# The last expert block's rows added on chip, and the last norm ahead of the overflow loop

## The chip, the cores and the metric

One core of a Trainium2 chip. The time is device microseconds for one execution of the whole program. Most executions of one kernel agree within 0.3%. Engines are TensorE (PE; its weight loads are PEld), VectorE (DVE), ScalarE (ACT), GpSimd (POOL) and SyncE (SP, which only issues DMAs here). DMAs are issued from the queues of SP, ScalarE and GpSimd.

## What is computed

One layer of a streaming encoder over 576 rows of 1024 channels: 512 rows of a new stream and 64 of a running one. After the token mixing and a first norm, each row is routed to two of 16 experts. The part that matters here is the end of it:

```
gl  = hf @ w_group + b_group ; g = argmax            # one group of 4 experts per row
top = top_k(router logits in the group, 2)           # two experts per row
act = silu(gate) * up * combine                      # each expert: 1024 -> 2 x 256
y   = sum over the row's two experts of act @ w_down # 256 -> 1024
x   = LayerNorm(ALPHA * x + (1 + g2) * y) * ln2_g + ln2_b
```

Everything is f32. The other outputs (keys, values, convolution state) are written long before.

## The kernel before

The 576 rows stand in five tiles of 128 rows (`TS` = 128, 128, 128, 128, 64). A scratch tensor in DRAM, `z_scr` (`z_d`), first receives ALPHA times the normed rows (`ax_rows`, line 888), and each expert's output is then added to it row by row.

**Units.** The experts are worked off by `units` (line 1276 on): four fixed ones, then nine by the string "mhhsmsmsm". Each letter stands for experts in order of how many rows they have: "h" is one expert in two blocks of 128 rows, "m" one expert in one block, "s" two small experts that share a block, 64 rows each. For each block `gather` fetches the rows with an indirect DMA, `rows_in` transposes them, `gate_up` multiplies them in four steps, `hidden` makes the activation. Within a loop over the units the block before is finished inside the steps of the present one: `turned` transposes the activation, `down` (lines 1175 and 1179) multiplies it with `w_down` into two PSUM banks `pd`, and `add_rows` (line 1182) multiplies by the gate on VectorE (line 1186, tile `yo`) and adds the result to `z_scr` by an indirect accumulating DMA from GpSimd (line 1190), whose row numbers stand in `idt`, `ido` or `cols`. A block of an "s" unit issues two of them, one for each expert; there are 18 in all. Each waits until the one before has landed, because rows of different experts may be the same rows.

**Buffers.** Seven large slots (`slot`) rotate: six hold the ring of expert weights, one the transposed rows `xhl`. What is allocated after them, as `rows3` (the last norm's gain and bias, line 1475), takes the slot of the oldest weights when those have been read.

**Order.** Inside `tc.manual_schedule` the order on TensorE, VectorE and ScalarE is the order in which the code is written; SP and GpSimd, and everything behind that block, are ordered by a planner with a timing model. An engine's instructions run in that order.

**The end.** After the last unit `turn_next` and `product_next` finish the pending block. Then comes the overflow loop (`tc.For_i`, line 1484), for experts that got more rows than their blocks hold. Its count is a value read at run time; in the profiled execution it is zero, and no line of its body is in the trace. Its entry and exit on every engine are checks of semaphores and branches. Behind the loop, for each of the five tiles: SP loads `zt` from `z_scr` (line 1515), the statistics are taken on VectorE for tile 0 (`stats`, `bn_stats` at line 804) and on ScalarE for the others (`act_stats`: a copy with a sum at line 1505, a square with a sum at 1507, a root at 1508, a reciprocal on VectorE at 1509), two VectorE passes (1517 and 1518) subtract the mean, multiply by gain and the inverse deviation and add the bias, and SP stores the tile (1519). The program's end has line 1560.

Of the kernel before, what the change touches and what calls it, by code (L numbers as in the profile page):

```python
# [10 lines left out]
F32 = mybir.dt.float32  # L11
# [3 lines left out]
AF = mybir.ActivationFunctionType  # L15
OP = mybir.AluOpType
AX = mybir.AxisListType

D = 1024
# [5 lines left out]
NT = 5  # L25
TS = [128, 128, 128, 128, 64]
# [14 lines left out]
NFIX = 4  # L41
# [8 lines left out]
def dap(a, offset, ap):  # L50
    return bass.AP(tensor=a.tensor, offset=a.offset + offset, ap=ap)
# [7 lines left out]
def encoder_step(ctx: ExitStack, tc: tile.TileContext, a, o):  # L59
    nc = tc.nc  # L60
    V, S, G, PE, SY = nc.vector, nc.scalar, nc.gpsimd, nc.tensor, nc.sync

    def scratch(name, shape, dt=F32):
        return nc.dram_tensor(name, shape, dt).ap()
# [4 lines left out]
    z_d = scratch("z_scr", (T, D))  # L69
# [7 lines left out]
    def slot(shape, dt=F32, name="slot"):  # L77
        return big.tile(shape, dt, name=name, tag="slot", padded_shape=None)
# [19 lines left out]
    ident = cst.tile([128, 128], F32, name="ident")  # L98
# [9 lines left out]
    epst = cst.tile([128, 1], F32, name="epst")  # L108
# [188 lines left out]
    class AdaRows:  # L297
# [12 lines left out]
        def product(self):  # L310
            k = self.done
            self.done += 1
            if k == 0:
                self.p = fifth(self.name)
            for j in range(4):
                PE.matmul(self.p[32 * j:32 * j + 32, :], cT[:, k, :], self.ws[k // 2][:, k % 2, 512 * j:512 * j + 512],
                          start=k == 0, stop=k == KT - 1, tile_position=(0, 32 * j))
# [12 lines left out]
    def fm(src, ncols, c0, xh, xl, m=128):  # L330
        with tc.high_priority(offset=400):
            raw = wcols(src, ncols, c0, m)
            ada_next("load")
            with tc.issue_after(hlast):
                w = split(raw, [128, KT, m])
        ps = [acc(), acc()]
        ada_next("product")
        for h in range(2):
            for k in range(KT):
                fm_step(ps, w, h, k, xh, xl, m)  # L340
        return ps
# [110 lines left out]
    def tm(c0, n, kstep):  # L452
        ps = [(acc, acc, acc, dot, fifth)[t](f"tm{t}") for t in range(NT)]
        for k0 in range(0, KT, kstep):
            with tc.high_priority():
                raw = wload(dap(a["w_in"], k0 * 128 * NIN + c0, [[NIN, 128], [128 * NIN, kstep], [1, n]]),
                            [128, kstep, n])
                wh, wl = split(raw, [128, kstep, n])
            order = [(k, t) for k in range(k0, k0 + kstep) for t in range(NT)]
            if k0 + kstep == KT:  # L460
                order = [(k, t) for t in range(NT) for k in range(k0, KT)]
            tokens_product(ps, k0, kstep, hh, hl, hs, wh, wl)
        return ps
# [25 lines left out]
    ps = fm(a["w_in"], NIN, C_KI, hh, hl, 72)  # L489
# [8 lines left out]
    for kv, t0, t1, n in ((kip, 0, 4, 128), (kis, 4, 5, DEC)):  # L498
        src = pki[0:n, 72 * t0:72 * t1].rearrange("p (t c) -> p t c", t=t1 - t0)
# [10 lines left out]
    ps = tm(C_QI, 512, 2)  # L510
    for t in range(NT):
        n = TS[t]
# [32 lines left out]
    ps = tm(C_K, 512, 2)  # L545
    for t in range(NT):
        n = TS[t]
# [17 lines left out]
    for c in range(2):  # L565
        ps = tm(C_Q + 512 * c, 512, 2)
        for t in range(NT):
            n = TS[t]
# [33 lines left out]
    bias = {0: bias0}  # L602
# [147 lines left out]
    late = ctx.enter_context(tc.tile_pool(name="late", bufs=2))  # L750


    def brow(dst, src, off, eng=G):
        eng.dma_start(dst, dap(src, off, [[0, 128], [1, D]]))
# [46 lines left out]
    def stats(src, n):  # L801
        bs = late.tile([128, 2, 6], F32, name="bs", tag="bs", bufs=2)
        for c in range(2):
            V.bn_stats(bs[0:n, c, :], src[0:n, 512 * c:512 * c + 512])
        mv = late.tile([128, 4], F32, name="mv", tag="mv", bufs=NT)
        V.bn_aggr(mv[0:n, 0:2], bs[0:n])
        S.activation(mv[0:n, 2:3], mv[0:n, 1:2], AF.Sqrt, bias=epst[0:n])
        V.reciprocal(mv[0:n, 2:3], mv[0:n, 2:3])
        return mv[0:n, 0:1], mv[0:n, 2:3]
# [3 lines left out]
    iota128 = late.tile([128, 128], F32, name="iota128", bufs=1)  # L813
# [35 lines left out]
    ps = [(acc, acc, acc, dot, fifth)[t](f"o{t}") for t in range(NT)]  # L849
# [117 lines left out]
    for t in range(NT):  # L967
        n = TS[t]
# [54 lines left out]
    for j in range(2):  # L1023
        V.tensor_tensor(Ej[:, j], Ej[:, j], bc(w12[:, :, j], 16), op=OP.mult)
        for t in range(NT):
            n = TS[t]
            PE.matmul(pwt[:, 0:16], ohr[0:n, j, t, :].bitcast(F32), Ej[0:n, j, t, :], start=t == 0 and j == 0,
                      stop=t == NT - 1 and j == 1)
# [6 lines left out]
    with tc.issue_after(routed):  # L1035
# [17 lines left out]
        cols = late.tile([128, 2, NVAR], F32, name="cols", bufs=1)  # L1053
# [94 lines left out]
    def hidden(p, w):  # L1148
        hm = late.tile([128, DE], F32, name="hm", tag="hm", bufs=3)
        S.activation(hm, p[:, 0:DE], AF.Silu)  # L1150
        V.scalar_tensor_tensor(hm, hm, w, p[:, DE:2 * DE], op0=OP.mult, op1=OP.mult)
        return hm

    def turned(hm):
        pt = fifth("pht")
        for i in range(2):
            PE.transpose(pt[:, 128 * i:128 * i + 128], hm[:, 128 * i:128 * i + 128], ident)
        hT = late.tile([128, 2, 128], F32, name="hT", tag="hT", bufs=2)
        S.copy(hT, pt[:, 0:256].rearrange("p (k t) -> p k t", k=2))  # L1159
        return hT  # L1160

    def gate_row(s0, s1):
        y = wp.tile([128, D], F32, name="yo", tag="wraw", bufs=2) if len(scatters) % 3 else \
            late.tile([128, D], F32, name="yo", tag="xg", bufs=2)
        S.activation(y, gr1, AF.Copy, scale=s1)
        V.scalar_tensor_tensor(y, gr0, s0, y, op0=OP.mult, op1=OP.add)
        return y
# [15 lines left out]
    def add_rows(y, pd_, ids):  # L1183
        for c in range(2):
            cs = slice(512 * c, 512 * c + 512)
            V.tensor_tensor(y[:, cs], y[:, cs], pd_[c], op=OP.mult)

        for i, idx in enumerate(ids):
            half = slice(128 // len(ids) * i, 128 // len(ids) * (i + 1))
            sc = G.indirect_dma_start(out=z_d, out_offset=bass.IndirectOffsetOnAxis(ap=idx[0:128 // len(ids)], axis=0),  # L1190
                                      in_=y[half], in_offset=None, bounds_check=T - 1, oob_is_err=False, compute_op=OP.add)
        scatters.append(sc.ins)
# [80 lines left out]

    plan = [[u] for u in range(NFIX)]
    nxt_ = {"h": 0, "m": NPAIR, "s": NFULL}
    for kind in "mhhsmsmsm":
        r = nxt_[kind]
        nxt_[kind] += 1
        plan.append([NFIX + r] + ([NFIX + r + NHALF] if kind == "s" else []))
    units, nb = [], 0  # L1280
    for es in plan:
        x = Unit()
# [12 lines left out]
    for u, x in enumerate(units):  # L1295
        x.experts = []
        for e in x.es:
            y = Expert()
# [67 lines left out]
    with tc.manual_schedule(engines={mybir.EngineType.PE, mybir.EngineType.DVE, mybir.EngineType.Activation}):  # L1366
# [4 lines left out]
        pend, over = [], overflow()  # L1371
# [10 lines left out]
        for u, x in enumerate(units):  # L1382
            if u == 2:
                for y in units:
                    i = y.es[0] - NFIX
# [8 lines left out]
            for b, _ in x.blocks:  # L1394
                p = Unit()
# [42 lines left out]
            def turn_next(i):  # L1438
                if i < len(pend):
                    pend[i].hT = turned(pend[i].hm)  # L1440

            def product_next(i):
                if i < len(pend):
                    product(pend[i])

            if len(blocks) == 1:
                p = blocks[0]
# [10 lines left out]
            else:  # L1458
                p, q = blocks
# [14 lines left out]
            pend = blocks  # L1474
        rows3 = slot([128, 2, D], name="rows3")
        brow(rows3[:, 0], a["ln2_g"], 0, SY)
        brow(rows3[:, 1], a["ln2_b"], 0, SY)
        for i in range(len(pend)):
            turn_next(i)
            product_next(i)  # L1480

    nvals = nc.values_load_multi_w_load_instructions(ovi[0:1, 2 * NOV:2 * NOV + 1], min_val=0, max_val=NOV,
                                                     skip_runtime_bounds_check_because="bounded by the counts")[1]
    with tc.For_i(0, nvals[0], 1) as i:
# [11 lines left out]
            load_down(ev, k, wt[1][:, k, :])  # L1496
        y = gate_row(s0, s1)
        add_rows(y, down(turned(hidden(pg, w)), [[wt[1][:, k, :] for k in range(2)]]), ids)


    jk = slot([128, D], name="jk")

    def act_stats(src, n):
        mv = late.tile([128, 4], F32, name="mv", tag="mv", bufs=NT)
        S.activation(jk[0:n], src[0:n], AF.Copy, scale=1.0 / D, accum_out=mv[0:n, 0:1])
        V.tensor_scalar(mv[0:n, 3:4], mv[0:n, 0:1], -1.0, None, op0=OP.mult)
        S.activation(jk[0:n], src[0:n], AF.Square, bias=mv[0:n, 3:4], accum_out=mv[0:n, 1:2])
        S.activation(mv[0:n, 2:3], mv[0:n, 1:2], AF.Sqrt, bias=epst[0:n], scale=1.0 / D)
        V.reciprocal(mv[0:n, 2:3], mv[0:n, 2:3])
        return mv[0:n, 0:1], mv[0:n, 2:3]  # L1510

    for t in range(NT):
        n, s = TS[t], int(t == 4)
        zt = slot([128, D], name="zt")
        SY.dma_start(zt[0:n], dap(z_d, t * 128 * D, [[D, n], [1, D]]))
        mean, rs = stats(zt, n) if t == 0 else act_stats(zt, n)
        V.scalar_tensor_tensor(zt[0:n], zt[0:n], mean, rows3[0:n, 0], op0=OP.subtract, op1=OP.mult)
        V.scalar_tensor_tensor(zt[0:n], zt[0:n], rs, rows3[0:n, 1], op0=OP.mult, op1=OP.add)
        SY.dma_start(dap(o["y"][s], (t % 4) * 128 * D, [[D, n], [1, D]]), zt[0:n])


# [42 lines left out]
```

## Time and profile before

| | us |
|---|---|
| median of 3 runs | 874.6 |
| lowest and highest | 872.26, 875.77 |
| the profiled execution's own time | 876.71 |
| its span | 875.0 |
| TensorE busy | 791.9 (90%) |
| VectorE busy | 640.5 (73%) |
| ScalarE busy | 358.6 (41%) |
| GpSimd busy | 143.6 (16%) |

The span is what the hardware profiler records; 1.7 us of the execution's time lie around it. Busy shares are averages over stages with different limits. The tail from about 830 us on is a stage of its own: there the chain of waits (at each step the thing that released the next) and the table by stretches say more than the shares. The mean granted clock of TensorE over the span is 0.95 of full speed.

### The profile page before, as it was taken

What the parts mean: (1) busy time and instruction counts of PE and PEld (TensorE: products, weight loads), DVE (VectorE), ACT (ScalarE), POOL (GpSimd) and SP (SyncE); (2) the same over time, 40 slices, a digit from 0 to 9 for tenths busy, and PEclk for the clock granted to TensorE, in tenths of its full rate; (3) what the DMA queues carried; (4) which work ended last, traced back from release to release, by engine and by line L of the source; (5) the groups of instructions that cost most, each with busy time, mean ns of one, the idle gap of its engine ahead of it and who ended that gap; (6) DMA issues with size and microseconds to landing.
All of it is one profiled execution on the core that took longest, in us unless ns stands there. A gap on an engine that the chain in (4) does not pass through costs nothing.

```text
span 875.0 us, 13257 instructions
## 1 busy us (share of the span) xinstructions
PE 791.9 (90%) x4827; PEld 640.9 (73%) x4827; DVE 640.5 (73%) x1255; ACT 358.6 (41%) x654; POOL 143.6 (16%) x172
## 2 busy tenths in 40 slices
PE   4899999999999999999999999799947999999920
PEld 3788888887878879879899789788836667645400
DVE  1569999989999889988896425437797697555516
ACT  3243232324344335547743852222433564344205
POOL 2300000310200000000100001020257532322220
PEclk9999999999999999999999999899956999999975
DMA  9997664491423224232443105677597999799525
GB/s 289 342 352 254 204 201 126 120 246 56 148 75 89 83 75 115 89 100 62 135 127 106 54 1 194 224 214 260 116 273 242 346 348 316 200 335 386 149 46 201
DMA packets 108866, 159.70 MB, mean 183 GB/s; under 512 B 9715, under 2 KB 67211, under 8 KB 108801
## 3 DMA queue, kind: packets, MB, share of 16 engines
q1 hardware_dynamic: 94464, 120.38, 42.1%
q0 software_dynamic: 12736, 34.26, 15.3%
q10 hardware_dynamic: 1600, 4.22, 1.3%
q8 instruction: 38, 0.62, 0.3%
q14 instruction: 28, 0.22, 0.1%
HBM read 143.65 MB, written 26.13 MB: 194 GB/s over the span
## 4 chain that ended last, share of the span: by engine, by line
PE 58%; DVE 7%; DMA 7%; issue 2%; ACT 2%; POOL 1%; POOLq 0%; SPq 0%; DVEq 0%; ACTq 0%
PE acc L242 7%; PE acc L244 7%; PE acc L243 7%; PE pd L1175 4%; PE pdot L528 3%; PE pg L1145 2%; DMA wraw<-in_w_att_out_dram 2%; PE tm L144 2%; PE tm L146 2%; PE tm L145 2%; PE pl L652 2%; PE po L660 2%; PE pg L144 2%; DMA z_scr<-yo,idt 2%; PE pg L146 2%
## 5 line engine op out<-in xcount | busy, mean ns | idle before, releaser
L588 DVE SCALAR_TENSOR_TENSOR y<-ue,dwT,y 128x604 f32<-128x604 f32 (+17 forms) x232 | 183.2, 828 | 1.9 <-ACT y L586 1.5
L242 PE MATMUL acc<-hh,wlo 128*128 128x288 f32 (+1 forms) x504 | 152.7, 304 | 1.6 <-DVE wlo L140 1.6
L243 PE MATMUL acc<-hh,whi 128*128 128x288 f32 (+1 forms) x504 | 150.4, 299 | 0.0
L244 PE MATMUL acc<-hl,whi 128*128 128x288 f32 (+1 forms) x504 | 149.3, 300 | 0.0
L139 ACT CAST whi<-wraw 128x1024 fp32r<-128x1024 f32 (+1 forms) x72 | 75.0, 1043 | 172.7 <-PE acc L244 85.5
L140 DVE TENSOR_TENSOR wlo<-wraw,whi 128x1024 fp32r<-128x1024 f32 (+1 forms) x72 | 87.4, 1214 | 52.6 <-ACT whi L139 52.3
L242 PEld LDWEIGHTS acc<-hh,wlo 128*128 128x128 f32 (+1 forms) x504 | 94.2, 187 | 17.5 <-issue 8.8
L243 PEld LDWEIGHTS acc<-hh,whi 128*128 128x128 f32 (+1 forms) x504 | 94.2, 187 | 5.2 <-issue 5.1
L244 PEld LDWEIGHTS acc<-hl,whi 128*128 128x128 f32 (+1 forms) x504 | 93.7, 187 | 5.5 <-issue 5.2
L144 PE MATMUL tm<-wlo,hh 128*128 128x512 f32 x128 | 50.5, 397 | 0.4 <-DVE wlo L140 0.4
L145 PE MATMUL tm<-whi,hh 128*128 128x512 f32 x128 | 50.4, 393 | 0.0
L146 PE MATMUL tm<-whi,hl 128*128 128x512 f32 x128 | 49.8, 392 | 0.0
L140 DVE TENSOR_TENSOR wlo<-ring,whi 128x1024 fp32r<-128x1024 f32 x30 | 36.3, 1222 | 13.2 <-ACT whi L139 13.0
L1175 PE MATMUL pd<-ring,hT 128*128 128x512 f32 x96 | 44.5, 607 | 1.0 <-ACT hT L1159 1.0
L242 PE MATMUL acc<-oh,wlo 128*128 128x288 f32 x128 | 39.4, 308 | 5.6 <-DVE gt L744 5.1
L139 ACT CAST whi<-ring 128x1024 fp32r<-128x1024 f32 x30 | 31.3, 1049 | 29.0 <-PE pg L146 25.4
L244 PE MATMUL acc<-yl,whi 128*128 128x288 f32 x128 | 39.3, 310 | 0.6 <-DVE yl L721 0.5
L1190 POOL DMA_INDIRECT z_scr<-yo,idt x16 | 28.3, 1769 | 68.6 <-DMA z_scr<-yo,idt 29.8
L244 PE MATMUL acc<-ol,whi 128*128 128x288 f32 x128 | 39.2, 309 | 0.0
L243 PE MATMUL acc<-oh,whi 128*128 128x288 f32 x128 | 39.1, 306 | 0.0
L243 PE MATMUL acc<-yh,whi 128*128 128x288 f32 x128 | 38.3, 301 | 0.0
L242 PE MATMUL acc<-yh,wlo 128*128 128x288 f32 x128 | 37.9, 297 | 0.0
(474 smaller groups left out, 1769.0 us busy)
## 6 DMA issues: line engine op xcount, KB each, us to landing
ring<-in_w_gate_up_dram SPq DMA_DIRECT2D x62, 512.0 KB, 8.5
wraw<-in_w_in_dram SPq DMA_DIRECT2D x48, 512.0 KB, 4.9
wada<-in_w_ada_dram SPq DMA_DIRECT2D x32, 512.0 KB, 6.0
ring<-in_w_down_dram SPq DMA_DIRECT2D x32, 512.0 KB, 10.6
wada<-in_w_ada_dram SPq DMA_DIRECT2D x32, 256.0 KB, 6.2
gates_scr<-glg POOLq DMA_DIRECT2D x16, 288.0 KB, 2.6
gt<-gates_scr POOLq DMA_DIRECT2D x16, 288.0 KB, 3.1
wraw<-in_w_conv_out_dram SPq DMA_DIRECT2D x8, 512.0 KB, 4.0
```

The source lines that it names most:

```text
L139: split_copy[0] = S.copy(hi, raw).ins
L140: V.tensor_tensor(lo, raw, hi, op=OP.subtract)
L144: PE.matmul(out, lh, rl, start=start, stop=False)
L145: PE.matmul(out, lh, rh, start=False, stop=False)
L146: PE.matmul(out, ll, rh, start=False, stop=stop)
L242: PE.matmul(ps[h][0:m, 0:288], wl[:, k, :], xh[:, k, sl], start=k == 0, stop=False)
L243: PE.matmul(ps[h][0:m, 0:288], wh[:, k, :], xh[:, k, sl], start=False, stop=False)
L244: return PE.matmul(ps[h][0:m, 0:288], wh[:, k, :], xl[:, k, sl], start=False, stop=k == KT - 1).ins
L528: PE.matmul(pdt[0:n, 0:L], qiT[pr, h // 2, 128 * t:128 * t + n], kiT[pr, k0:k0 + L], start=True, stop=True)
L588: V.scalar_tensor_tensor(y[:, 30 - i:EXT], ue[:, 0:EXT - 30 + i], dwT[:, j, i:i + 1], y[:, 30 - i:EXT], op0=OP.mult, op1=OP.add)
L1175: PE.matmul(pd_[c], hT[:, k, :], dns[0][k][:, cs], start=k == 0, stop=k == 1)
L1190: sc = G.indirect_dma_start(out=z_d, out_offset=bass.IndirectOffsetOnAxis(ap=idx[0:128 // len(ids)], axis=0), in_=y[half], in_offset=None, ...
```

## The change

The unit order becomes "mhhsmssmm". After the last unit, the row numbers of its block are turned into five matrices of 128x128, `oht`: in column r of matrix t, a one in the place of the block's row that belongs to row 128 t + r. The five tiles `zt` are loaded from `z_scr` at this point of the program, ahead of the last block's product and of its addition to `z_scr`, which is still made. Then, for each tile, TensorE adds in PSUM the loaded rows (a product with the identity) and the last block's rows (a product of `oht` with `p.y`), in two halves of 512 columns, and the norm is made from PSUM: tiles 0 and 3 with `bn_stats` on VectorE, tiles 1, 2 and 4 with copies, sums and squares on ScalarE. All this stands ahead of the overflow loop. The loop's body ends with loads of all five tiles and the whole norm again, so that rows that overflow are counted.

```diff
-    for kind in "mhhsmsmsm":
+    for kind in "mhhsmssmm":
...
-        for i in range(len(pend)):
-            turn_next(i)
-            product_next(i)
+        e, = units[-1].es
+        oht = slot([128, NT, 128], name="oht")
+        for t in range(NT):
+            V.tensor_scalar(oht[:, t, :], iota128, 128.0 * t + 1.0, cols[:, 0, e - NFIX:e - NFIX + 1], op0=OP.add, op1=OP.is_equal)
+        zts = [slot([128, 4, D], name="zt"), slot([128, D], name="zt")]
+        zt = [zts[0][:, t, :] for t in range(4)] + [zts[1]]
+        for t in range(NT):
+            SY.dma_start(zt[t][0:TS[t]], dap(z_d, t * 128 * D, [[D, TS[t]], [1, D]]))
+        p, = pend
+        turn_next(0)
+        product_next(0)
+    def finish(t, x, neg, rs):
+        n, s = TS[t], int(t == 4)
+        for src, c0, c1 in x:
+            V.scalar_tensor_tensor(zt[t][0:n, c0:c1], src[0:n], neg, rows3[0:n, 0, c0:c1], op0=OP.add, op1=OP.mult)
+        V.scalar_tensor_tensor(zt[t][0:n], zt[t][0:n], rs, rows3[0:n, 1], op0=OP.mult, op1=OP.add)
+        SY.dma_start(dap(o["y"][s], (t % 4) * 128 * D, [[D, n], [1, D]]), zt[t][0:n])
+    def act_stats(src, n, sums):
+        mv = late.tile([128, 4], F32, name="mv", tag="mv", bufs=NT)
+        V.tensor_scalar(mv[0:n, 0:1], sums[0:n, 0:1], sums[0:n, 1:2], -1.0 / D, op0=OP.add, op1=OP.mult)
+        S.activation(jk[0:n], src[0:n], AF.Square, bias=mv[0:n, 0:1], accum_out=mv[0:n, 1:2])
+        S.activation(mv[0:n, 2:3], mv[0:n, 1:2], AF.Sqrt, bias=epst[0:n], scale=1.0 / D)
+        V.reciprocal(mv[0:n, 2:3], mv[0:n, 2:3])
+        return mv[0:n, 0:1], mv[0:n, 2:3]
+    def sums_of(parts, n):
+        sums = late.tile([128, 2], F32, name="sums", tag="nm", bufs=2)
+        for i, (dst, src) in enumerate(parts):
+            S.activation(dst[0:n], src[0:n], AF.Copy, accum_out=sums[0:n, i:i + 1])
+        return sums
+    banks = [(acc, acc), (acc, fifth), (trp, trp), (dot, dot), (acc, acc)]
+    halves = [(0, 512), (512, D)]
+    for t in range(NT):
+        n = TS[t]
+        ps = [bank("pz") for bank in banks[t]]
+        for q, (c0, c1) in zip(ps, halves):
+            PE.matmul(q[0:n], ident[0:n, 0:n], zt[t][0:n, c0:c1], start=True, stop=False)
+        for q, (c0, c1) in zip(ps, halves):
+            PE.matmul(q[0:n], oht[:, t, 0:n], p.y[:, c0:c1], start=False, stop=True)
+        if t in (0, 3):
+            ...
+            finish(t, [(q, c0, c1) for q, (c0, c1) in zip(ps, halves)], mv[0:n, 3:4], mv[0:n, 2:3])
+        else:
+            sums = sums_of([(zt[t][:, c0:c1], q) for q, (c0, c1) in zip(ps, halves)], n)
+            finish(t, [(zt[t], 0, D)], *act_stats(zt[t], n, sums))
...
     with tc.For_i(0, nvals[0], 1) as i:
         ...
-    for t in range(NT):
-        ...
+        for t in range(NT):
+            n = TS[t]
+            SY.dma_start(zt[t][0:n], dap(z_d, t * 128 * D, [[D, n], [1, D]]))
+            finish(t, [(zt[t], 0, D)], *act_stats(zt[t], n, sums_of([(jk[:, c0:c1], zt[t][:, c0:c1]) for c0, c1 in halves], n)))
```

## Rows read from the trace of the kernel before

**Rows 1.** Stretches of the tail, busy time of each engine (table by windows).

```profile
core 0: us, PE busy (x) PEld busy (x) DVE busy (x) ACT busy (x) POOL busy (x), PEclk, DMA share, GB/s
838.00:850.00 12.00, 0.00 (x0) 0.00 (x0) 0.09 (x1) 0.00 (x0) 2.98 (x2) 0.69 0.23 35
850.00:860.00 10.00, 0.00 (x0) 0.00 (x0) 4.25 (x8) 4.17 (x8) 0.00 (x0) 0.50 0.70 236
860.00:875.00 15.00, 0.00 (x0) 0.00 (x0) 10.66 (x16) 7.71 (x15) 0.00 (x0) 0.50 0.42 157
```

**Rows 2.** Chain that ended last: start us, us, what.

```profile
814.43 3.44 PE pd L1175 x8
...
840.14 3.47 DMA z_scr<-yo,idt
...
844.35 5.70 DMA z_scr<-yo,idt
...
850.70 3.76 DMA zt<-z_scr
...
854.48 1.30 DVE bs L804 x2
...
869.71 1.28 DVE zt L1518
```

**Rows 3.** Waits of GpSimd from 744 to 850: us in total, times, longest.

```profile
POOL z_scr L1190 <- DMA z_scr<-yo,idt: 38.6, 7, 8.9
```

**Rows 4.** Timeline of TensorE: start us, us, line, tiles [idle before <-releaser].

```profile
557.43 0.61 PE L242 MATMUL acc<-oh,wlo 128*128 128x288 f32 x1 [5.06 <-DVE gt L744]
...
558.32 0.44 PE L242 MATMUL acc<-oh,wlo 128*128 128x288 f32 x1
558.55 0.44 PE L243 MATMUL acc<-oh,whi 128*128 128x288 f32 x1
...
562.61 0.30 PE L242 MATMUL acc<-oh,wlo 128*128 128x288 f32 x1
562.74 0.30 PE L243 MATMUL acc<-oh,whi 128*128 128x288 f32 x1
...
833.66 3.70 PE L1175 MATMUL pd<-ring,hT 128*128 128x512 f32 x8 [0.52 <-ACT hT L1159]
```

**Rows 5.** Two stretches by windows, columns as in rows 1 (PEclk third from last).

```profile
562.00:564.00 2.00, 2.00 (x15) 2.00 (x15) 0.76 (x2) 0.75 (x1) 0.00 (x0) 0.86 0.32 122
...
842.00:844.00 2.00, 0.00 (x0) 0.00 (x0) 0.00 (x0) 0.00 (x0) 0.00 (x0) 0.61 0.34 43
```

**Rows 6.** Instructions on the tile `zt`: durations in ns, minimum/median/maximum.

```profile
L1517 DVE SCALAR_TENSOR_TENSOR zt<-zt,mv,rows x5: 1277/1285/1285, 856.0 to 868.3; 128x1024 f32<-128x1024 f32 x4, 64x1024 f32<-64x1024 f32 x1
...
L804 DVE BATCH_NORM_STATS2 bs<-zt x2: 677/686/694, 854.5 to 855.1; 128x6 f32<-128x512 f32 x2
```

**Rows 7.** Timeline of VectorE and ScalarE, single pieces, columns as in rows 4.

```profile
757.54 1.07 ACT L1130 COPY xw<-pxt 128x512 f32<-128x512 f32 x2
...
834.69 1.29 DVE L1166 SCALAR_TENSOR_TENSOR yo<-gr,sel,yo 128x1024 f32<-128x1024 f32 x1 [2.04 <-ACT yo L1165]
...
837.40 0.69 DVE L1186 TENSOR_TENSOR yo<-yo,pd 128x512 f32<-128x512 f32 x1 [0.63 <-PE pd L1175]
...
867.05 1.15 ACT L1507 ACTIVATE jk<-zt,mv 64x1024 f32<-64x1024 f32 x1 [0.21 <-DVE mv L1506]
868.10 0.19 ACT L1507 ACTIVATION_READ_ACCUMULATOR jk<-zt,mv 64x1 f32 x1
868.32 0.29 ACT L1508 ACTIVATE mv<-mv,epst 64x1 f32<-64x1 f32 x1
...
869.52 0.15 DVE L1509 RECIPROCAL mv<-mv 64x1 f32<-64x1 f32 x1
```

**Rows 8.** Instructions of line 1484 (the loop's entry and exit) on SP, ns.

```profile
L1484 SPq EVENT_SEMAPHORE  x20: 17/28/4209, 810.5 to 850.5; - x20
```

**Rows 9.** Instructions of line 1560 (the program's end) on SP, ns.

```profile
L1560 SPq DRAIN  x3: 7/7/7, 874.1 to 874.4; - x3
```

More of the change, by code (lines that the diff above doesn't have):

```diff
@@ new lines, in encoder_step @@
+    jk = slot([128, D], name="jk")
+    def act_stats(src, n, sums):
[5 more added lines that the diff above has]
+        return mv[0:n, 0:1], mv[0:n, 2:3]
@@ new lines, in sums_of @@
+    def sums_of(parts, n):
[13 more added lines that the diff above has]
+        if t in (0, 3):
+            bs = late.tile([128, 2, 6], F32, name="bs", tag="bs", bufs=2)
+            for i in range(2):
+                V.bn_stats(bs[0:n, i, :], ps[i][0:n])
+            mv = late.tile([128, 4], F32, name="mv", tag="mv", bufs=NT)
+            V.bn_aggr(mv[0:n, 0:2], bs[0:n])
+            S.activation(mv[0:n, 2:3], mv[0:n, 1:2], AF.Sqrt, bias=epst[0:n])
+            V.tensor_scalar(mv[0:n, 3:4], mv[0:n, 0:1], -1.0, None, op0=OP.mult)
+            V.reciprocal(mv[0:n, 2:3], mv[0:n, 2:3])
+            finish(t, [(q, c0, c1) for q, (c0, c1) in zip(ps, halves)], mv[0:n, 3:4], mv[0:n, 2:3])
+        else:
+            sums = sums_of([(zt[t][:, c0:c1], q) for q, (c0, c1) in zip(ps, halves)], n)
+            finish(t, [(zt[t], 0, D)], *act_stats(zt[t], n, sums))
@@ L1498, in encoder_step @@
         add_rows(y, down(turned(hidden(pg, w)), [[wt[1][:, k, :] for k in range(2)]]), ids)
[L1501 to L1510, printed above, removed]
-    for t in range(NT):
[L1513 to L1519, printed above, removed]
+        for t in range(NT):
+            n = TS[t]
+            SY.dma_start(zt[t][0:n], dap(z_d, t * 128 * D, [[D, n], [1, D]]))
+            finish(t, [(zt[t], 0, D)], *act_stats(zt[t], n, sums_of([(jk[:, c0:c1], zt[t][:, c0:c1]) for c0, c1 in halves], n)))
 _INS = ["x_prompt", "x_sample", "cache_k", "cache_v", "cache_idx_k", "state_conv", "c_prompt", "c_sample",
```

## The prediction

> **What bounds the kernel now.** I read the stretch table of the tail first, then the chain of waits, then who holds GpSimd's queue. The table says that from 838 to 850 us no compute engine does anything, and that from 850 to the end TensorE is idle while VectorE and ScalarE do the last norm [rows 1]. The chain names the reason: the last row updates of `z_scr` run one behind the other (one of 3.47 us from 840.14, the last of 5.70 from 844.35, landed at 850.05), only then come the loads of `zt` (issued 850.70, the first lands 3.76 later), and then the norm of five tiles, whose last VectorE instruction ends at 869.71 + 1.28 = 870.99 [rows 2]. The last product has been over since 833.66 + 3.70 = 837.4 [rows 4], so the updates, not TensorE, set the start of the norm. They have done so for long: from 744 on GpSimd waits 38.6 us in 7 waits for the update before [rows 3]. A busy share of 90% for TensorE over the span hides this; the tail alone tells what the change is worth.
>
> **Part 1, the last update leaves the chain.** The one-hot product needs `z_scr` as the first 17 updates left it. The new unit order "mhhsmssmm" issues the same kinds of update as before, and the one that leaves is a whole block's. Since they queue without a gap, their order hardly matters to the end of the seventeenth: 840.14 + 3.47 = 843.6, which I take, with 1.5 us to either side, because the pairs and the single blocks now meet other transfers. Each y is ready in time: the last unit's is complete at 837.40 + 0.69 = 838.1 and its update goes out at 844.35, 6 us later [rows 2, 7]; the second-last unit's is ready a whole unit earlier. The SP issue behind the loop's closing checks, 850.70 - 850.05 = 0.65, is gone from this place too [rows 2]. So the loads go out at 843.7 instead of 850.70, 7.0 us earlier, and the first tile is there at 843.7 + 3.76 = 847.5. All five take 10 us or less (236 GB/s over 10 us is the 2.36 MB of five tiles) [rows 1], and they stay ahead of what follows.
>
> The eighteenth update is still made, now behind the loads: it overwrites what they read, so GpSimd's queue holds it until the fifth load has landed, about 853. Behind it on that queue is only the entry of the overflow loop, and it lands some 6 us later, among the first stores of y. That is hidden by a norm that lasts to 870; without that cover it would cost its 5.70 [rows 2]. On SP the loads wait at the head, and what is queued behind them is stores that need them anyway. `rows3` takes the slot of weights that a pair now reads to its end, so its two loads go out about one unit later; it is needed only at about 853.
>
> **Part 2, the one-hot columns and the moved unit.** Five comparisons of 128x128 are new on VectorE just ahead of the last product. The nearest row is 0.69 for 128x512, so at most 3.5 us, against 2.04 us in which VectorE is idle there [rows 7]. The up to 1.4 us that spill over only delay `p.y`, which TensorE asks for after 847: nothing. Swapping a pair and a single unit keeps TensorE's work, and a stall of some us there would be absorbed by the 6 us and more for which every y waits for its turn.
>
> **Part 3, what TensorE now does in the tail.** Per tile there are four products (two halves of the rows through the identity, two of the one-hot columns with y), 128 rows by 512 columns in plain f32, 20 in all. The nearest row is the down product, `down()`, which has the same shape and type: its four calls are 8 matmul records and last 3.44 us at the full clock, so 0.86 a call [rows 2]. But the clock is not full there: it fell to 0.5, the 1.2 GHz level, between 842 and 844, after TensorE had been idle since 837.4 [rows 4, 5]. In the new kernel the same idle stretch ends only at 847.5. At that level the starts of equal matmuls lie 0.23 apart where they lie 0.13 apart later [rows 4], so a call costs 1.72. The return can be read at 557: TensorE starts at 557.43 after 5.06 us idle and the clock comes back in the stretch from 562, at about 562.6, 5.1 us later [rows 4, 5]. So 847.5 to 852.6 holds three calls, and the other seventeen take 14.6: TensorE ends at 867.2. One tile takes 3.44 of them, more than the 2.9 of VectorE for one tile now (two of 1.28 and two small ones) [rows 6, 7]: **TensorE, idle until now, paces the tail.** With a full clock all along it would end 2.6 us sooner.
>
> The Trainium skill's page "TensorE: Matmul & The Clock Gate", section "Loop structure matters more than you think", advises against just this: it shows matmuls behind a long DMA wait as the pattern in which the array goes cold. The trace agrees with its fall at 842 to 844; were that rule not to hold here, the sum below would be 2.6 us less.
>
> **Part 4, the norm itself.** Tiles 0 and 3 go by VectorE (two statistics of 0.69, halves of 0.69 from PSUM, one of 1.28, small ones: 4.6 us). Tiles 1, 2 and 4 go by ScalarE: two copies with sums (0.54 each plus 0.19 for the sum), a square of 1.15 + 0.19, a root of 0.29; on VectorE the reciprocal of 0.15, one small one and two of 1.28, so 2.9 [rows 6, 7]. Behind TensorE's end, tile 4 needs a copy 0.73, a small one 0.15, the square 1.34, the root 0.29, the reciprocal 0.15, the last pass 1.28 and some 0.3 of handovers: 867.2 + 4.2 = 871.4. VectorE is a little later: when tile 3's sums are complete, at 863.8, it still owes one pass of tile 2 (1.28), tile 3 (4.6) and tile 4 (2.9), less the 0.4 of tile 3 that it can begin before: 872.2. I take 872.3, against 870.99 now: **1.3 us later**, although the norm starts 7 us earlier.
>
> **Part 5, the closing.** The loop's entry and exit checks now stand behind the last store. After the store's landing SP now goes straight to its drain (874.1) and the span ends at 875.0 [rows 9]; afterwards it walks its 20 checks of about 0.03 first [rows 8]. Nearest row: seven of them took the 0.65 above. Bounds 0 (all but the last were met before) and 2.0 (all 20 at that spacing). I take 1.5, nearer the upper end, since SP's own resets can only be made after its stores have landed.
>
> **The sum**, against the profiled execution (876.7 us, span 875.0): VectorE's end +1.3, closing +1.5: +2.8, so 879.5 there; on the median of 874.6, **877.4 us**.
>
> **The rivals.**
> (a) *VectorE takes the tiles one after another.* Behind the hand-written part a planner orders VectorE and ScalarE. If it holds tile t+1's statistics and copies behind tile t's last pass, VectorE waits for ScalarE's copies, square and root (0.73 + 1.34 + 0.29, less one pass of 1.28: 1.1) in each of the three ScalarE tiles, and 0.3 for the root in tiles 0 and 3. That is 3.8 us more: 881.2, slower. It decides from 1.6 us of such waits. For it: nothing in the old tail shows PSUM tiles in that order. Against: now VectorE runs passes of one tile while ScalarE squares the next, 10.66 of 15 us busy [rows 1].
> (b) *A call costs one matmul record, 0.43.* Then VectorE paces: 17.9 us of work from 850.1 with 0.6 of gaps, end 868.6, 3.7 less: 873.7. Against: 8 records for four calls [rows 2].
> (c) *The change doesn't reach the loads.* They still wait for the eighteenth update, which is put ahead of them: 6.4 us later (850.1 for 843.7): 883.8. Against: they stand ahead of it in the program.
> (d) *The closing is free:* 875.9, and with the updates 1.5 us earlier 874.4. These lie within the forecast's own range.
>
> **How the numbers follow.** The forecast has 0.60 (alone 874.4 to 879.5: closing 0 to 2.0, updates 1.5 either way, the clock's return 0.9 either way), (a) 0.27, (b) 0.07, (c) 0.06. The range of 873.0 to 882.5 leaves out (c) and the far ends of (a) and (b). 0.5%, about what a measurement here can tell, is 4.4 us: faster means below 870.2, slower above 879.0. Faster needs (b) together with the early ends of all else: 0.04. Slower is (a) and (c) and a little of the forecast, less the mild form of (a): 0.34. Same: 0.62.
>
> **What would show it.** Right: loads issued near 843.7; half clock for the first products and TensorE dense from 847 to 867; VectorE's last pass ending near 872; the chain of waits naming the new products; the loop's checks behind the last store. Wrong: loads after 846 (part 1), TensorE done before 862 (part 3), gaps of over 1 us on VectorE between tiles (rival a), a closing of under 1.5 us in all (part 5).

## The result and the profile after

| | before | after |
|---|---|---|
| median, us (7 runs each, same chip) | 873.55 | 883.43 |
| lowest and highest | 868.73, 875.77 | 878.4, 888.3 |
| profiled execution's own time | 876.71 | 881.53 |
| its span | 875.0 | 879.8 |

The ratio is 1.0123 with an interval of 1.0083 to 1.0163: the changed kernel is slower by 0.8 to 1.6%. Single executions spread wider here than the 0.3% named above suggests: of 35 of the kernel before, beside one of the runs below, 21 lie within 0.3% of their median, and all of them within 867.41 to 877.35, which is 1.1%. Forecast were 877.4 and at most 882.5.

The chain of waits after, for the tail (start us, us, what), against [rows 2]:

```profile
838.87 5.97 DMA z_scr<-yo,idt
...
845.01 3.46 DMA zt<-z_scr
848.47 0.04 issue
848.52 1.98 PE pz L1521 x4
...
853.08 2.59 PE pz L1523 x6
...
855.69 0.16 ACT zt L1512
...
870.35 1.28 DVE zt L1496
```

One update has left the chain: the loads are issued at 845.01 where they were at 850.70. The new products are in the chain, as forecast, but only to 853.08 + 2.59 = 855.67; behind that it names ScalarE and VectorE alone. VectorE ends at 870.35 + 1.28 = 871.63, where it ended at 870.99. The stretches of the tail, columns as in [rows 1]:

```profile
838.00:850.00 12.00, 7.69 (x24) 3.75 (x23) 4.15 (x10) 1.80 (x3) 1.57 (x1) 1.00 0.48 140
850.00:860.00 10.00, 10.00 (x25) 4.47 (x24) 5.24 (x10) 4.97 (x12) 1.57 (x1) 1.00 0.45 120
860.00:875.00 15.00, 6.52 (x14) 1.52 (x12) 11.43 (x19) 5.18 (x13) 0.00 (x0) 0.86 0.44 161
```

VectorE, which ends at 871.63, is busy for 11.43 of the last 11.63 us before that. TensorE, which had nothing to do from 838 on before, is busy for 7.69 us of the first stretch. That is not the new work alone. Its timeline shows the last down product late, and where the lateness began (columns as in [rows 4]):

```profile
798.60 2.08 PE L1175 MATMUL pd<-ring,hT 128*128 128x512 f32 x2 [7.41 <-ACT hT L1159]
...
842.02 3.70 PE L1175 MATMUL pd<-ring,hT 128*128 128x512 f32 x8 [0.52 <-ACT hT L1159]
848.52 1.98 PE L1521 MATMUL pz<-zt,ident 128*128 128x512 f32 x4 [2.80 <-DMA zt<-z_scr]
...
865.45 1.07 PE L1523 MATMUL pz<-yo,oht 128*64 128x512 f32 x2
```

The last down product ends at 842.02 + 3.70 = 845.72; in [rows 4] it ended at 837.36. Of these 8.4 us, 7.41 are one gap, in which TensorE waits for ScalarE's copy `hT`. ScalarE's timeline says what held the copy:

```profile
797.23 1.04 ACT L139 CAST whi<-ring 128x1024 fp32r<-128x1024 f32 x1 [10.45 <-DMA ring<-in_w_gate_up_dram]
798.18 0.37 ACT L1159 COPY hT<-pht 128x256 f32<-128x256 f32 x1
```

The copy takes 0.37 us and stands in ScalarE's fixed order behind a cast of weights that had not landed. The cast is the split (into a high and a low part) of the weights of the second-last unit, a single block since the change. A pair needs no split, so `split_ahead` reached past the two pairs ahead of it. The DMA engines had little room to bring the weights sooner. Over 780 to 798 they move

```profile
DMA packets 2963, 6.78 MB, mean 376 GB/s; under 512 B 467, under 2 KB 467, under 8 KB 2961
```

with a busy share of 0.9 or more in nearly every slice. Behind the 7.41 us without work TensorE's granted clock is 0.50 (1.2 GHz) too, as the stretch from 796 to 802 shows:

```profile
796.00:802.00 6.00, 3.40 (x4) 1.51 (x5) 1.75 (x2) 2.92 (x5) 0.00 (x0) 0.50 0.44 146
```

So an update came late, as GpSimd's timeline shows (the eleventh and twelfth update, then the sixteenth to the eighteenth):

```profile
794.00 1.43 POOL L1190 DMA_INDIRECT z_scr<-yo,idt  x1 [6.19 <-DMA z_scr<-yo,idt]
806.45 1.57 POOL L1190 DMA_INDIRECT z_scr<-yo,idt  x1 [11.02 <-DVE yo L1186]
...
834.58 1.41 POOL L1190 DMA_INDIRECT z_scr<-yo,idt  x1 [3.40 <-DMA z_scr<-yo,idt]
838.87 1.57 POOL L1190 DMA_INDIRECT z_scr<-yo,idt  x1 [2.89 <-DVE yo L1186]
855.10 1.57 POOL L1190 DMA_INDIRECT z_scr<-yo,idt  x1 [14.65 <-DMA zt<-z_scr]
```

The twelfth belongs to the product behind the gap. It waits for its own y, complete at 806.2, though the eleventh had landed at 794.00 + 6.1 = 800.1: 6 us are lost. The thirteenth loses 1.4 us more in the same way (its y at 817.1, the twelfth landed at 815.7). Since each update waits for the one before, all that follow inherit the loss. The seventeenth adds nothing to it, although the profile puts its 2.89 us of idle time down to its y: that was complete at 838.03, and the sixteenth landed at 834.58 + 3.6 = 838.2, within 0.2 us of it. In before, where the last y was complete 6 us ahead, GpSimd stood idle as long at that place:

```profile
844.35 1.57 POOL L1190 DMA_INDIRECT z_scr<-yo,idt  x1 [2.80 <-DMA z_scr<-yo,idt]
```

The eighteenth waits 14.65 us for the loads and then runs under the norm.

The closing, from VectorE's last instruction to the end of the span, is 8.2 us (871.6 to 879.8); before, it was 4.05. In after the last store of line 1497 is issued at 871.7 and lands up to 2.9 us later (instructions of that line: shortest/median/longest in ns, first and last start; then its DMAs):

```profile
L1497 SPq DMA_DIRECT2D out_dram<-zt x5: 332/338/499, 859.5 to 871.7; - x5
...
DMA to landing us min/median/max: 2.7/2.8/2.9
```

What follows is set by GpSimd's drain at the program's end. The first three rows are from after (the loop's branches on SP and GpSimd, then the drains), the fourth is from before:

```profile
L1541 SPq COMPARE_BRANCH  x3: 38/43/58, 872.6 to 875.7; - x3
L1541 POOLq COMPARE_BRANCH  x3: 38/41/53, 855.3 to 874.9; - x3
```
```profile
L1600 POOLq DRAIN  x3: 51/109/3709, 875.1 to 879.4; - x3
```
```profile
L1560 POOLq DRAIN  x3: 51/109/3709, 850.9 to 874.8; - x3
```

The long one, 3.71 us, is the first of the three in both kernels. Before, it ran at 850.9 beside the norm, since GpSimd was through with everything once the loop was left. Now GpSimd leaves the loop at 874.9, after the last store has landed, and its drain runs from 875.1 to 878.8, with nothing beside it from 876 on. SP's own checks are over at 875.7, 1.1 us behind the landing (871.7 + 2.9 = 874.6).

### The profile page after: what moved, and what is told of

The parts are those of the page before. It is cut to its first block, busy times and chain, and to the rows that moved or that the text cites. A ratio compares the mean times of both kernels' runs of the same rounds, so it can differ in the third digit from the quotient of the medians.

```text
span 879.8 us, 13371 instructions
## 1 busy us (share of the span) xinstructions
PE 810.0 (92%) x4867; PEld 647.6 (74%) x4867; DVE 642.8 (73%) x1266; ACT 356.6 (41%) x656; POOL 139.8 (16%) x172
## 5 line engine op out<-in xcount | busy, mean ns | idle before, releaser
L1175 PEld LDWEIGHTS pd<-ring,hT 128*128 128x128 f32 x96 | 18.1, 198 | 29.2 <-issue 17.5
L1190 POOL DMA_INDIRECT z_scr<-yo,idt x16 | 25.4, 1585 | 82.9 <-DVE yo L1186 35.8
```

The costliest lines, as they stand in the source:

```text
L1175: PE.matmul(pd_[c], hT[:, k, :], dns[0][k][:, cs], start=k == 0, stop=k == 1)
```

## The experiments

Two theories stood at first. *The stall:* the new unit order puts the split ahead of the copy, and the 7.4 us push the updates and with them the loads. *The closing:* the loop behind the norm puts the loop's checks and GpSimd's drain at the end of the program. The rivals were that one of the two explains all, or that TensorE's work in the tail does. Later runs ask what that work costs, and whether the terms add up.

The profiled executions differ by some us in when the updates land. So the table also gives two lengths inside the tail, "tail" from the issue of the first load of `zt` to VectorE's last instruction, and "closing" from there to the end of the span. "End" is the end of the span, counted from the first matmul of line 1145 (at 760.7 before, 759.9 after), as the expectations count.

| kernel | median, us | ratio to before, interval | tail | closing | end |
|---|---|---|---|---|---|
| before | 870.8 to 876.7 | 1 | 20.3 | 4.1 | 114.4 |
| after | 883.43 | 1.0123 (1.0083 to 1.0163) | 26.6 | 8.2 | 120.0 |
| order_back | 879.82 | 1.0078 (1.0040 to 1.0115) | 29.2 | 8.2 | 117.9 |
| order_alone | 879.62 | 1.0068 (1.0026 to 1.0111) | 20.2 | 4.1 | 117.5 |
| split_late | 880.77 | 1.0077 (1.0035 to 1.0119) | 28.1 | 8.2 | 115.7 |
| no_loop | 885.00 | 1.0131 (1.0067 to 1.0195) | 29.2 | 4.0 | 124.3 |
| late_no_loop | 872.11 | 1.0011 (0.9981 to 1.0042) | 28.1 | 4.0 | 115.1 |
| onehot_first | 872.03 | 0.9997 (0.9968 to 1.0025) | 24.3 | 8.2 | 115.2 |
| loop_first | 872.90 | 1.0023 (0.9992 to 1.0054) | 29.2 | 4.1 | 112.9 |
| loop_first_oh | 872.55 | 1.0011 (0.9987 to 1.0035) | 29.0 | 4.1 | 117.1 |
| warm_alone | 875.23 | 0.9986 (0.9955 to 1.0017) | 26.4 | 4.1 | 112.6 |
| warm_first | 878.03 | 1.0000 (0.9971 to 1.0030) | 24.6 | 4.1 | 112.8 |
| onehot_no_loop | 868.29 | 0.9946 (0.9906 to 0.9987) | 22.7 | 4.0 | 105.9 |
| before_no_loop | 869.53 | 0.9991 (0.9964 to 1.0019) | 20.4 | 3.9 | 110.3 |

Medians of different rows come partly from different chips, so only the ratios compare them.

### The stall: order_back, order_alone, split_late

**order_back** is the changed kernel with the old order.

```diff
-    for kind in "mhhsmssmm":
+    for kind in "mhhsmsmsm":
```

> The changed kernel with the old unit order mhhsmsmsm; everything else of the change stays. Theory 1 (ScalarE's split of the second-last unit's weights is queued ahead of their landing and holds TensorE some 8 us): the 10 us wait of ScalarE near 797 is gone, the last product ends at about 837 instead of 846, loads of zt go out at 843.7 instead of 845.0, but TensorE is then idle for 10 us and the first products run at 1.2 GHz, so the norm ends at 872, as now; the median falls by 3 to 6 us because the spread that the stall brings is gone. Rival (the product and the norm alone cost it all): wait or not, the median stays within 1.5 us of the changed kernel's, 883.

**order_alone** is the kernel before with the new order alone (the same diff the other way round).

> The kernel before with the new unit order mhhsmssmm alone. Theory 1: ScalarE waits some 10 us near 787 to 797 for a landing, the last product ends 8 us later, near 846, and the last update goes out at 846.6 instead of 844.4: 2 to 6 us slower than the kernel before. Rival (the order is neutral, since every y waits 6 us for its turn): within 1 us of the kernel before.

**split_late** keeps the new order; the second-last unit's splits are issued one for each step of the pair ahead of it.

```diff
     def split_ahead():
         ...
+            if x is units[11] and now[0] * 4 + now[1] < 40 + c:
+                return
...
             def freed(c):
+                now[:] = [u, c]
```

> The changed kernel, in which the second-last unit's splits on ScalarE and VectorE are written one per step of the pair before it, instead of as early as buffers allow. Theory 1: ScalarE's wait near 797 shrinks under 1 us, TensorE has no gap over 1.5 us between 700 and 838, and the rest goes as in the kernel with the old order (loads 843.7, norm end 872, median 3 to 6 us below the changed kernel). Rival (the pair's weights themselves come late): TensorE still has a gap of several us there, the releaser being a ring load.

The order alone, with nothing of the new norm, makes the kernel before slower by 0.3 to 1.1%. Its rows of TensorE and ScalarE are those of after:

```profile
799.43 2.08 PE L1175 MATMUL pd<-ring,hT 128*128 128x512 f32 x2 [7.33 <-ACT hT L1159]
```
```profile
798.06 1.04 ACT L139 CAST whi<-ring 128x1024 fp32r<-128x1024 f32 x1 [10.37 <-DMA ring<-in_w_gate_up_dram]
```

In split_late, with the same order but the cast moved, the same product follows its transposes without a gap, and ScalarE's copy waits for nothing but them:

```profile
793.89 3.60 PE L1175 MATMUL pd<-ring,hT 128*128 128x512 f32 x8
```
```profile
793.27 0.37 ACT L1159 COPY hT<-pht 128x256 f32<-128x256 f32 x1 [3.62 <-PE pht L1157]
```

So it is the place of the cast in ScalarE's order, not the order of the units as such. The loads go out at 840.5 in order_back and 842.2 in split_late. But most of the loss stays: 1.0078 and 1.0077. Going by the middle values the stall is 0.45% of the 1.23%, some 3.9 us. The intervals of after and of order_back overlap, and a difference of that size is not clear of noise: that the order costs time is shown by order_alone, how much of it the changed kernel pays is an estimate. Part of what its removal gains goes back at once, for TensorE is now idle long enough before the rows land that its clock falls. First the stretches of split_late, then one of after:

```profile
844.00:846.00 2.00, 0.14 (x1) 0.14 (x1) 0.00 (x0) 0.00 (x0) 0.00 (x0) 0.50 0.96 367
846.00:848.00 2.00, 2.00 (x3) 0.97 (x4) 0.00 (x0) 0.00 (x0) 0.00 (x0) 0.50 1.04 412
848.00:850.00 2.00, 2.00 (x4) 0.79 (x4) 0.00 (x0) 0.00 (x0) 0.00 (x0) 0.72 0.99 307
```
```profile
848.00:850.00 2.00, 1.48 (x4) 0.77 (x5) 0.00 (x0) 0.00 (x0) 0.00 (x0) 1.00 0.94 367
```

In split_late TensorE had been idle for 6.96 us and begins at 0.50 (the 1.2 GHz level); in after it had been idle for 2.80 and keeps 1.00. The tail is 28.1 and 29.2 us where it is 26.6 in after: the fall costs 1.5 to 2.6 us.

### The closing: no_loop, late_no_loop, before_no_loop

All three leave the overflow loop out; with these inputs its body never runs.

```diff
-    nvals = nc.values_load_multi_w_load_instructions(...)[1]
-    with tc.For_i(0, nvals[0], 1) as i:
-        ...
```

**no_loop** is the changed kernel without it, **late_no_loop** is split_late without it, **before_no_loop** the kernel before without it.

> The changed kernel without the overflow loop (its count is zero here, so the outputs are the same): that part of the computation is left out. Theory 2 (the loop's exit and GpSimd's drain of 3.7 us stand behind the last store): from VectorE's end to the span's end 4.0 us instead of 8.2, so 4 us less than the changed kernel in the median; GpSimd's drain comes before 862. Rival (the drain belongs to the indirect updates and ends the program in any case): under 1.5 us less.

> The kernel of split_late with the overflow loop left out (no expert overflows with these inputs). Closing theory: between VectorE's last instruction and the end of the span lie 4.0 us instead of the 8.2 of split_late, since GpSimd's drain of 3.7 us has no instruction of the loop's exit ahead of it and runs earlier; counted from the first matmul of line 1145 the span ends at 111.5 instead of 115.7, against 114.4 in the kernel before, so a time about 4 us below split_late, ratio to before 0.997 to 1.003. Rival, the closing is set by the stores' landing whatever stands behind them: 8 us stay, ratio 1.007 as for split_late.

> The kernel before with the overflow loop left out: the base with which onehot_no_loop (0.9946) has to be compared. In the kernel before, the loop stands between the landing of the last update and the loads and cost 0.65 us there, and GpSimd's drain was hidden: so the time falls by 0.7 us or less, ratio 0.998 to 1.001, closing 4.0. Rival, the loop costs the kernel before as much as the norm's closing costs the changed one (4 us, by what the loop keeps the planner from putting earlier): ratio 0.994 to 0.997, and then onehot_no_loop owes its gain to the missing loop.

The closing is 4.0 us in no_loop and late_no_loop. GpSimd's long drain of late_no_loop begins at 852.1, with the eighteenth update under way, and lasts 8.17 us, until 860.2, all of it under the norm:

```profile
L1583 POOLq DRAIN  x3: 51/110/8165, 852.1 to 874.1; - x3
```

no_loop's time did not fall, against the expectation. Its profiled execution has a larger stall (8.16 and 2.38 us on TensorE), and its interval is wide enough to hold the expected fall of 4 us, so by its time it decides nothing:

```profile
801.17 6.49 PE L1175 MATMUL pd<-ring,hT 128*128 128x512 f32 x8 [8.16 <-ACT hT L1159]
818.30 3.65 PE L1179 MATMUL pd<-ring,hT 128*64 128x512 f32 x16 [2.38 <-ACT hT L1159]
```

late_no_loop, which has no stall, is the clean pair with split_late: 1.0077 to 1.0011, 0.66% or 5.8 us by the middle values, 4.2 us by the closings in the profile. (The two were measured on different chips, each beside before; why the times differ by more than the closings is open.) In the kernel before, the loop costs nothing that can be measured (0.9991). It is its place behind the norm that costs.

### TensorE's products in the tail: onehot_first, loop_first, loop_first_oh, warm_alone, warm_first, onehot_no_loop

**onehot_first** is split_late with the one-hot products of tiles 0 to 3 issued first, so that they run while the rows are being loaded:

```diff
+    pss = [one_hot(t) for t in range(4)]
     for t in range(NT):
+        ps = pss[t] if t < 4 else one_hot(t)
         for q, (c0, c1) in zip(ps, halves):
-            PE.matmul(q[0:n], ident[0:n, 0:n], zt[t][0:n, c0:c1], start=True, stop=False)
-        for q, (c0, c1) in zip(ps, halves):
-            PE.matmul(q[0:n], oht[:, t, 0:n], p.y[:, c0:c1], start=False, stop=True)
+            PE.matmul(q[0:n], ident[0:n, 0:n], zt[t][0:n, c0:c1], start=False, stop=True)
```

> The kernel of split_late with the one-hot products of tiles 0 to 3 issued ahead of all identity products (the sum in PSUM starts with them), so that 8 of the 20 products run while the rows are still being loaded. If TensorE's 20 products, the first at half clock, pace the tail: from the issue of the first load to VectorE's last instruction 22 to 24 us instead of 28.1 (eight products of 0.86 and the half clock are taken out of the wait, after which VectorE paces), time 4 to 5 us below split_late, ratio to before 0.996 to 1.002. Rival, VectorE and ScalarE pace the tail by themselves: at most 1.5 us less (26.6 or more), ratio 1.006.

```profile
835.86 7.03 PE L1525 MATMUL pz<-yo,oht 128*128 128x512 f32 x16
846.40 8.72 PE L1533 MATMUL pz<-zt,ident 128*128 128x512 f32 x16 [3.51 <-DMA zt<-z_scr]
```

Eight products (16 records) run from 835.86 on, under the landing of the seventeenth update and of the rows; the tail falls from 28.1 to 24.3 us, a little above what was expected, and the ratio from 1.0077 to 0.9997. The ratio falls by 0.8%, some 7 us, the tail by 3.8 us; the two were measured on different chips, and the rest is open. So TensorE paced the tail of split_late, where the chain of waits stays on it to 860.6; in after it left TensorE at 855.67. The half clock did not go: after 3.51 us of idle time the granted clock is 0.56 from 846 to 848. With eight products gone VectorE paces, as the stretch from 850 to its end shows, busy for 15.70 us of 17:

```profile
850.00:867.00 17.00, 9.13 (x20) 2.66 (x19) 15.70 (x27) 9.61 (x24) 1.57 (x1) 0.89 0.45 145
```

**loop_first** keeps all that is computed: the old unit order, 17 updates and no eighteenth, then the loop (its body without loads and norm), then loads and norm once.

```diff
-            add_rows(p.y, p.pd, p.ar[0])
+            add_rows(p.y, p.pd, [] if last else p.ar[0])
...
-        zts = [slot([128, 4, D], name="zt"), slot([128, D], name="zt")]
-        ...
         turn_next(0)
-        product_next(0)
+        product(p, True)
+    with tc.For_i(0, nvals[0], 1) as i:
+        ...
+    zts = [slot([128, 4, D], name="zt"), slot([128, D], name="zt")]
+    ...
```

> The units in the order of the kernel before; 17 updates, and the eighteenth is not made; the overflow loop stands between the seventeenth update and the loads of the five tiles, and the norm with the one-hot products is there once, behind the loop. Closing theory: GpSimd's drain and the loop's checks lie under the norm again, so 4.05 us from VectorE's last instruction to the end. Loads at 81 counted from the first matmul of line 1145 (order_back 80.5, and 0.65 for the loop's exit), 29 us to VectorE's last instruction, with half clock for the first products: end at 113 to 114.5 against 114.4 before, ratio 0.994 to 1.002. Rival, the closing stays at 8 us because the norm, not the loop, makes it: ratio 1.007. Rival, the loop's exit costs the loads over 2 us, because all engines must come to it: loads at 83 or later, ratio 1.003 to 1.008.

**loop_first_oh** is loop_first with the one-hot products first, as in onehot_first.

> loop_first with the one-hot products of tiles 0 to 3 ahead of the identity products. If TensorE paces the tail: 23 to 25 us from load to VectorE's last instruction, which comes at 104 to 106 counted from the first matmul of line 1145 (before: 110.3), end at 108 to 110 against 114.4, ratio 0.992 to 0.996, which would be the fastest version. If VectorE and ScalarE pace it by themselves: as loop_first, 0.994 to 1.002.

The closing is 4.1 us in both, with the same norm behind the loop: the loop's place makes the 8 us, not the norm. GpSimd's long drain stands at 837.2, under the loads:

```profile
L1597 POOLq DRAIN  x3: 51/109/3627, 837.2 to 870.0; - x3
```

loop_first is no faster than before (1.0023, just outside what was expected); its tail has the half clock again (29.2 us). loop_first_oh missed its expectation: TensorE cannot pass the loop until the seventeenth update has landed, so in this place its one-hot products begin at 844.4, 0.6 us after the loads were issued, and only delay the first tile (tail 29.0).

**warm_alone** is loop_first with eight products that nobody reads, five ahead of the loop and three behind it.

```diff
+    def warm(count):
+        q = dot("idle")
+        for _ in range(count):
+            PE.matmul(q, ident, oht[:, 0:4, :], start=True, stop=True)
+    warm(5)
...
+    warm(3)
```

> loop_first with eight products of 128x128 by 128x512 added whose results nobody reads: five between the last down product and the loop, three behind the loop, so that TensorE isn't idle for long before the rows land. If the half clock of the first products is what makes the tail 29.2 us in loop_first (26.6 in the changed kernel, where the clock was full): granted clock 1.0 for all the norm's products and 26 to 27 us from the first load to VectorE's last instruction, closing 4.1, ratio to before 0.997 to 1.000. Rival, the first products wait for the rows of later tiles and not for the clock: 29 us as before, ratio 1.002; if the five products hold up the loop's exit, the loads come later than in loop_first by as much.

The first product on the rows then runs at full clock: it follows work with no gap, four records in 1.98 us, where the same four take 3.78 in loop_first. First warm_alone, then loop_first:

```profile
837.97 2.84 PE L1492 MATMUL idle<-oht,ident 128*128 128x512 f32 x6 [1.99 <-issue]
840.67 1.98 PE L1548 MATMUL pz<-zt,ident 128*128 128x512 f32 x4
```
```profile
840.52 3.78 PE L1541 MATMUL pz<-zt,ident 128*128 128x512 f32 x4 [6.42 <-DMA zt<-z_scr]
```

The tail is 26.4 us, as in after: full clock is worth 2.8 us there. By the times (0.9986) it can't be told from before, nor surely from loop_first.

**warm_first** joins the two: three unread products and the one-hot products of tile 0 ahead of the loop, those of tiles 1 and 2 behind it, ahead of the identity products, with the PSUM banks dealt out for that.

> loop_first with the one-hot products of tile 0 and three unread products ahead of the loop, those of tiles 1 and 2 right behind the loop ahead of the identity products, and the PSUM banks of tiles 1 to 3 dealt out otherwise for that. TensorE theory: full clock, six of the 20 products out of the wait for the rows, 22 to 24.5 us from the first load to VectorE's last instruction (29 in loop_first and loop_first_oh, 24.3 in onehot_first), closing 4.1: end at 106 to 110 counted from the first matmul of line 1145, against 114.4 before; ratio 0.992 to 0.997, faster than both kernels. Rival, the tail is bound by VectorE and ScalarE once the rows are there: 26 us or more and a ratio of 0.999 to 1.002.

The tail is 24.6 us, just over what was expected, but the ratio of 0.992 to 0.997 was missed: the time is that of the kernel before. Three tiles' one-hot products (the planner put tile 3's there too) stand between the loop and the first identity product, which starts at 852.1, 5.8 us after the loads were issued.

**onehot_no_loop** is onehot_first without the overflow loop.

> onehot_first (splits spread out, one-hot products of tiles 0 to 3 ahead of the identity products) with the overflow loop left out as well. If the three terms found are separate and add up (stall 0.45%, closing 0.66%, products behind the loads 0.8%): 24.3 us from the first load to VectorE's last instruction, closing 4.0, ratio to before 0.9997 - 0.005 to 0.0066, so 0.993 to 0.996. If the closing is only hidden behind something else once the norm is shorter (GpSimd's drain and the landing of the eighteenth update, which ended at 860 in late_no_loop): ratio 0.997 to 1.000.

0.9946 lies inside the 0.993 to 0.996 expected of terms that add up, though its interval reaches into the rival's 0.997 to 1.000, and its tail is 1.6 us shorter than the 24.3 us expected. It is faster than before, by 0.1 to 0.9%. The right base for it is before_no_loop (0.9991), and there the intervals overlap: a gain of some 0.45% by the middle values is likely, not shown. It leaves the loop out, so it is no replacement; no version that keeps the loop was measurably faster than the kernel before.

## Why the prediction was wrong

Forecast were +2.8 us. Measured were 9.9 by the medians and 10.7 by the ratio. Of the 7 to 8 us between, 2.6 are a closing term that was too small and some 3.9 a stall that was set at nothing; the rest, about 1, stays unassigned, within the intervals. The pair of profiles shows less (VectorE's end +0.6, closing +4.1, in all +4.8), since the execution profiled of before lay 3.2 us above its median and that of after 1.9 below.

**Part 1 right, with little to spare.** The last update left the chain, and the eighteenth ran hidden. The loads came at 845.0 for the forecast 843.7. Without the stall they came at 840.5 (order_back) and 842.2 (split_late), for 842.2 to 845.2 with the bounds.

**Part 2 wrong at one sentence**, "a stall of some us there would be absorbed by the 6 us and more for which every y waits for its turn". The stall was 7.4 us, and the product behind it ran at half clock (5.69 us for 8 records, 3.60 in split_late). The twelfth update lost 6 us beyond its slack, the thirteenth 1.4, and the loads inherited it through the queue of updates. The 6 us had been read at the last update; the stall struck six updates earlier, and no size was worked out for it. The rows that could have given one were to be had: a fixed order on ScalarE, casts that stand in it as soon as a buffer is free, and DMA engines that are full in that stretch in before as well (372 GB/s from 780 to 798). The comparisons for the one-hot columns were cheap, as said, five of 0.28 us for a bound of 3.5 in all:

```profile
L1482 DVE TENSOR_SCALAR oht<-iota,cols x5: 281/281/282, 840.9 to 841.7; 128x128 f32<-128x128 f32 x5
```

**Part 3 right in the price of a call, wrong about the clock, for the reason of part 2, and only partly right that TensorE paces the tail.** The 20 products took from 848.52 to 866.52, 0.90 each for the forecast 0.86, and ended 0.7 us ahead of the forecast 867.2. At full clock they stayed ahead of VectorE: the chain leaves TensorE at 855.67, after eight of the calls (tiles 0 and 1), and from 860 on VectorE is hardly ever idle. Where the clock fell, in order_back and split_late, TensorE paced the tail to 860, as forecast. In after the clock did not fall, since the stall had moved TensorE's last work to 845.72. In order_back and split_late it fell as forecast and cost 1.5 to 2.6 us (2.8 by warm_alone; forecast 2.6). The Trainium skill's rule on matmuls behind a long DMA wait ("TensorE: Matmul & The Clock Gate", "Loop structure matters more than you think") therefore held in the runs in which the wait was long (6.96 us idle) and had no case in after, where it was 2.80.

**Part 4 right in its number, in part by luck.** VectorE ended 871.63 - 866.52 = 5.1 us behind TensorE, for 872.3 - 867.2 = 5.1. But tile 3 was complete at 860.64 + 1.88 = 862.5 (forecast 863.8):

```profile
860.64 1.88 PE L1523 MATMUL pz<-yo,oht 128*128 128x512 f32 x4
```

From there VectorE needed 9.1 us for the forecast 8.5, and TensorE 4.0 us for tile 4, forecast 3.4. The two misses cancel.

**Part 5 wrong in what ends the program:** +4.1 for +1.5, beyond its bound of 2.0. SP's checks were sized nearly right: they were over 1.1 us behind the landing. The step left out the other engines that pass the same exit. GpSimd's drain of 3.71 us stood in the trace of before, at 850.9, hidden; [rows 9] shows SP's drain only. Part 1 had followed GpSimd's queue, but only to "the entry of the overflow loop". What the moved loop holds back is what GpSimd does behind its exit.

**The rivals.** None came true. (c) gave 883.8, next to the measured time, but its mechanism was not there: the loads went out ahead of the eighteenth update. (a), 881.2, needed VectorE to wait for ScalarE between tiles; once tile 0's statistics were made, its longest such wait was 0.5 us. (b) had VectorE pace, as it did from 855.67 on, but for a reason that was not there: a call took two records.

## What to carry to other kernels

When a step is moved to the end of a program, list for each engine what it does last and what then runs behind the moved step; a drain that was hidden counts in full. Slack that is read at the last piece of a queue says nothing of the pieces ahead of it. When the order of work units changes, follow each prefetch to the queue in which its first consumer stands: a cast that waits for a DMA holds back everything behind it on that engine. A product put on an idle engine is cheap only if it can run while the data is still on its way.

## What was not expected of the hardware

GpSimd's first drain at the program's end took 3.71 us both in before, where its last update had landed 0.8 us earlier, and in after, where that was 14 us earlier (3.63 in loop_first). With an update still under way it took 8.17 (late_no_loop). The drains of SP beside it took 7 ns each.
